# Moving the constants behind a weight tile, shortening the zero products, and eight more pairs by seven products in an fp32 hybrid block

## The chip, the cores and the metric

The kernel runs on one core of one Trainium2 chip. The metric is the device time of one execution in microseconds, the median over runs; lower is better. The core has a matrix engine (TensorE; PE in the profile, its weight loads PEld), a vector engine (VectorE, DVE), a scalar engine (ScalarE, ACT), GpSimd (POOL) and SyncE (SP), whose queue issues nearly all transfers from memory. Each engine works off its own instructions in a fixed order.

## The reference

One layer of a sequence model over 256 positions of width 2048, all in float32, cut to what matters:

```python
def rms_norm(x, w):
    y = x * rsqrt(mean(x * x, axis=-1, keepdims=True) + 1e-6)
    return y * w

def hybrid_token_mixer(n, w_in, ...):
    proj = n @ w_in            # 2048 x 8208: q, k, v, z, a, b of eight gated DeltaNet heads,
                               # q, f, i, g of eight HGRN2 heads
    y_a = gated_deltanet_group(...)   # short causal convolution, l2 norms, chunked delta rule, gated norm
    y_b = hgrn2_group(...)            # lower-bounded forget gate, chunkwise recurrence, gated norm
    return concatenate([y_a, y_b], axis=-1) @ w_out       # 2048 x 2048

def squared_relu_mlp(n, w1, w2):
    return square(relu(n @ w1)) @ w2                      # 2048 x 8192, 8192 x 2048

def reference(x, ...):
    h = x
    h = h + hybrid_token_mixer(rms_norm(h, norm_mix_w), ...)
    h = h + squared_relu_mlp(rms_norm(h, norm_ffn_w), w_ff1, w_ff2)
    return rms_norm(h, norm_final_w)
```

## The kernel before

**Products in three parts.** TensorE multiplies in a rounded float32 format (F32R). A float32 matrix is therefore split in two: `hi`, its rounded copy, made by a cast on ScalarE (L120), and `lo`, the remainder `w - hi`, made on VectorE (L121). A product is then three matmuls, hi x hi, lo x hi and hi x lo (L805, L806, L807). Every weight goes through `split` on its way from memory, so each weight tile of 128 x 2048 costs ScalarE two casts and VectorE two remainders of 128 x 1024.

**Start.** The parameters come by the queue of ScalarE, everything else by that of SP: `x` transposed in eight pieces (tile `big`) and the first two weight tiles in eight pieces, one after the other (L146, L147). While they travel, GpSimd sets 384 columns of `sums` to zero and TensorE multiplies zeros, eight products of 128 x 128 with 128 x 256 into the tile `warm` (L173 to L175). `to_T` (L167, L168) then makes `xT`, the hi and lo of `x` times the norm weight.

**Projections.** `project` makes two outputs of one head from two weight tiles, `kh` 0 and 1. The first call (`first`) uses the two tiles that are already on their way. The second call (`second`) loads its tile `kh` 0 in four pieces and then, before its tile `kh` 1, three constants: `cst`, which holds the identity and two columns (L297), `cst_a` with the ones, masks and selections (L298), and `wab`, the weights of the gates (L299). Weight tiles have three buffers (`wpool`). Between the second call's splits stand the squares of `x` (`squares`), and after them the row sums by a product with the ones (`row_scales`). `parameters` copies the ones into `ones_r` in F32R, and `gates` splits `wab` and multiplies it with `xT` (tile `pab`). Then the heads follow, projections of one head beside the mixing of the one before, up to about 490 us.

**MLP.** A step takes a pair of k-tiles: one weight tile of 128 x 2048, which is a 2 x 2 block of parts of 128 x 512, against a 2 x 2 block of activations of 128 x 128, for two halves of the positions and two of the columns. There are two kinds.

- A plain pair (`plain_quad`): eight products, 24 matmuls, added into four accumulators `E`. Its weights take two splits of 128 x 1024.
- A pair by sums (`sum_quad`): seven products of sums of the parts (a Strassen-Winograd scheme), 21 matmuls, added into three of the `E` and four further accumulators `M`. VectorE makes the sums of the weights in the tile `TT`, which has one buffer (L845, L848, L849), and there are three splits of 128 x 1024 and one of 128 x 512. After the last pair of this kind `joins` adds the `M` together into `C4` (L863 to L867).

The split weights of 128 x 1024 have five buffers in turn (`split_pair`: three of one pool, two of another). The accumulators are the eight banks of PSUM, four of `acc_a` and four of `acc_b`; a group has its `E` in the one and its `M` in the other, and the next group the other way round.

The first product has eight groups `ng` of 1024 columns, each with eight pairs `kp`, three of them by sums (`SUMS`, pairs 2, 4 and 6). Its activations are made once: `blocks(kp, ...)` transposes a pair's part of `h` and writes either the plain hi and lo (`a_plain`) or the seven sums' hi and lo (`a_sums`). At a group's end VectorE adds each `E` to its part of `C4` (L906) and ScalarE takes the Relu (L907). Four `turn`s, one per quarter, then transpose these results (L817) and square them into `g` (L819). They wait in the list `fills` and are put between the next group's products: `fill(2)` after pair 0, and two in the middle of pair 1. The transposes go to banks of the pool that held the group's `E`, which is the pool of the next group's `M`.

The second product has two halves `q` of 1024 columns, each with 32 pairs, six of them by sums (`SUMS2`, pairs 3, 7, 11, 15, 19 and 23). The splits of `g` are made pair by pair (`a2_plain`, `a2_sums`). After the last pair by sums come `joins` and four additions into `h` (`add_to_h`), in the second half also the weighting of half of the first rows of the output (`weighted`). The last two pairs of a half are held and worked off accumulator by accumulator (`finish`), and the final norm is made piece by piece behind them.

**What sets the order.** The program text gives the priority, and a scheduler with a cost model writes each engine's order from it ahead of the run: an instruction that is lower in the text goes ahead where the model has the engine idle. On the chip each engine keeps to that order.

Of the kernel before, what the change touches and what calls it, by code (L numbers as in the profile page):

```python
# [15 lines left out]
P = 128  # L16
T = 256
# [58 lines left out]
def hybrid_block(ctx: ExitStack, tc: tile.TileContext, x, xt, w_in, w_ab, params, w_out, w_ff1, w_ff2,  # L76
# [93 lines left out]


    warm = mx("warm")
    POOL.memset(sums[:, 0:P + T], 0.0)  # L173
    for _ in range(8):
        PE.matmul(warm[:, 0:T], lhsT=sums[:, 0:P], rhs=sums[:, P:P + T], start=True, stop=True)  # L175

    for k in range(KT):
        to_T(xT, k, x3[:, k, :], cols[:, k:k + 1])

    def squares(c, after):  # L180

        t = junk if c else sums
        DVE.tensor_copy(t[:, 0:1], after)
        ACT.activation(t, big[:, c * 1024:(c + 1) * 1024], AF.Square)
        if c:
            DVE.tensor_tensor(out=sums, in0=sums, in1=junk, op=ALU.add)

    def row_scales():

# [14 lines left out]
        ACT.activation(u, u, AF.Exp, scale=-1.0)  # L204
        ACT.activation(u, u, AF.Ln, bias=1.0)

    ones_r = cpool.tile([P, P], F32R, tag="ones_r", name="ones_r")

    def parameters():

        DVE.tensor_copy(ones_r, ones)
        l0, l1 = cols[:, 34:42], cols[:, 42:50]
        DVE.tensor_tensor(out=par[:, 2, :], in0=l0, in1=l1, op=ALU.max)
        DVE.tensor_tensor(out=par[:, 3, :], in0=l0, in1=par[:, 2, :], op=ALU.subtract)
        DVE.tensor_tensor(out=par[:, 4, :], in0=l1, in1=par[:, 2, :], op=ALU.subtract)
        ACT.activation(par[:, 3:5, :], par[:, 3:5, :], AF.Exp)
        DVE.tensor_tensor(out=par[:, 5, :], in0=par[:, 3, :], in1=par[:, 4, :], op=ALU.add)
        DVE.reciprocal(par[:, 5, :], par[:, 5, :])
        DVE.tensor_tensor(out=lb, in0=par[:, 3, :], in1=par[:, 5, :], op=ALU.mult)
        DVE.tensor_scalar(oml, lb, -1.0, 1.0, ALU.mult, ALU.add)  # L220
        DVE.tensor_scalar(gnw[:, 0:1], cols[:, 32:33], float(P) ** -0.5, None, ALU.mult)
        DVE.tensor_copy(gnw[:, 1:2], cols[:, 33:34])
# [61 lines left out]
    def project(base, hd, chunk, dsts):  # L284
        second = base == 0 and hd == 0 and chunk == 1
        accs = [acc_a() for _ in range(2)]
        for kh in range(2):
            first = base == 0 and hd == 0 and chunk == 0
            if first:
                w = w_first[kh]  # L290
            else:
                w = wtile()
                src = w_in[((base > 0) * NH + hd) * 4 + chunk * 2 + kh]
                if second and kh == 0:
                    for c in range(4):
                        SP.dma_start(w[:, c * 512:(c + 1) * 512], src[:, c * 512:(c + 1) * 512])
                    SP.dma_start(cst, consts[:, 0:NKEEP])  # L297
                    SP.dma_start(cst_a, consts[:, NKEEP:])  # L298
                    SP.dma_start(wab, w_ab)  # L299
                else:  # L300
                    SP.dma_start(w, src)
            for q in range(2):
                hi, lo = split(w[:, q * 1024:(q + 1) * 1024], 1024, pieces=2 if first or second and kh == 0 else 1)
                if second:
                    squares(2 * kh + q, lo[:, 0:1].bitcast(F32))
                hi = hi.rearrange("p (k g c) -> p k g c", k=4, g=2)
                lo = lo.rearrange("p (k g c) -> p k g c", k=4, g=2)
                for kk in range(4):
                    k = kh * 8 + q * 4 + kk
                    for g in range(2):  # L310
                        PE.matmul(accs[g], lhsT=hi[:, kk, g, :], rhs=xT[:, k, :], start=(k == 0), stop=False)  # L311
                        PE.matmul(accs[g][:, T:], lhsT=lo[:, kk, g, :], rhs=xT[:, k, 0:T],  # L312
                                  start=False, stop=(k == KT - 1))
# [394 lines left out]


    KP = KT // 2  # L710
    SUMS = (2, 4, 6)
    sets = bpool.tile([P, 8192], F32R, tag="xT", name="sets")
    sets2 = tp.tile([P, 2 * 1792], F32R, tag="s2", name="sets2")
    plain = [kp for kp in range(KP) if kp not in SUMS]

    def a_plain(kp):
        n = plain.index(kp)
        return sets[:, n * 1024:(n + 1) * 1024].rearrange("p (k s) -> p k s", k=2)

    def a_sums(kp):  # L720
        t, at = (sets, 6144) if kp == SUMS[0] else (sets2, (SUMS.index(kp) - 1) * 1792)
        return t[:, at:at + 1792].rearrange("p (s n t) -> p s n t", s=2, n=7)

    h = hpool.tile([P, 2 * D], F32, tag="h", name="h").rearrange("p (f c) -> p f c", f=2)
# [14 lines left out]
    def blocks(kp, acc):  # L739
# [7 lines left out]
        if kp in plain:  # L747
            for kk in range(2):
                to_T(a_plain(kp), kk, pt[:, kk * T:(kk + 1) * T], wc[kk])
            return  # L750

        X = op.tile([P, 8, P], F32, tag="X", name="X", bufs=2)
# [118 lines left out]
    for ng in range(NGR):  # L871
# [2 lines left out]
        bank_e, bank_m = (acc_a, acc_b) if ng % 2 == 0 else (acc_b, acc_a)  # L874
        E = [bank_e() for _ in range(4)]
        M = None
        for kp in range(KP):
            w = wtile()
            SP.dma_start(w, w_ff1[ng * KP + kp])
            if kp not in SUMS:  # L880
                st = a_plain(kp)
                plain_quad(E, lambda kk, hf: [st[:, kk, c + hf * P:c + hf * P + P] for c in (0, T)], plain_weights(w),
                           kp == 0, kp == KP - 1, 0 if kp == 0 else 2)
                if kp == 0:
                    fill(2)
                if ng == 0 and kp == 1:
                    for hf in range(2):
                        DVE.tensor_tensor(out=fs[:, 4 + hf:5 + hf], in0=fs[:, 2 * hf:2 * hf + 1],
# [9 lines left out]
            if M is None:  # L898
                M = [bank_m() for _ in range(4)]
            st = a_sums(kp)  # L900
            sum_quad(E, M, [(st[:, 0, n, :], st[:, 1, n, :]) for n in range(7)], w, kp == SUMS[0], kp == SUMS[-1])
            if kp == SUMS[-1]:
                C4 = joins(M)

        for at, p in ((0, E[0]), (2, E[1]), (1, E[2]), (3, E[3])):
# [45 lines left out]
            DVE.tensor_scalar(h[:, hf, a:b], o[hf][:, a:b], s, None, ALU.mult)  # L951
        (ACT if eng is ACT else SP).dma_start(out[0, hf * P:(hf + 1) * P, a:b], h[:, hf, a:b])

    SUMS2 = (3, 7, 11, 15, 19, 23)
    TAIL = 2
    KP2 = NF // 2

# [142 lines left out]
```

## Time and profile before

| | |
|---|---|
| median of 3 runs | 1238.5 us (1237.87 to 1238.79) |
| profiled execution | 1239.85 us |
| its span, first to last instruction | 1238.1 us |
| granted TensorE clock, mean | 0.993 |
| TensorE busy | 1219.7 us, 7076 matmuls |
| VectorE busy | 1022.4 us |
| ScalarE busy | 767.2 us |
| GpSimd busy | 135.3 us |
| moved by transfers | 233.46 MB, 189 GB/s on average |

Rows of the profile name an engine, a line of the kernel, an operation and its tiles, written `out<-in`. In a list by time the first number is the start in microseconds from the span's start, the second the duration; `x2` says that two were merged. In brackets stands how long the engine had been idle, and what ended that. A row of the stretches gives, after its length, the busy time and count of instructions of TensorE, its weight loads, VectorE, ScalarE and GpSimd, then the granted clock, the share of the transfer engines and their GB/s. In lists of groups the two numbers behind the bar are the time in which at least one of the group ran, in us, and the mean duration in ns. In lists of waits they are the total in us, how often, and the longest.

### The profile page before, as it was taken

To read this page: it belongs to the slowest core of one execution; us is meant where nothing else is said; L and a number is where in the kernel's file an instruction comes from. 1 tells how busy PE (TensorE), PEld (TensorE's weight loads), DVE (VectorE), ACT (ScalarE), POOL (GpSimd) and SP (SyncE) were. 2 spreads that over 40 slices of the span, in tenths; PEclk is the share of its full clock that TensorE was granted. 3 is DMA by queue.
4 is the path that set the end of the run, shared out by engine and by line. 5 is a ranking of instruction groups with operands and counts; after the bars stand their busy time and mean duration, and the time that the engine had idled before them with its cause. 6 is when DMAs were issued, how large, how long until landed. Compare 5 with 4: busy or idle time off the path is not lost.

```text
span 1238.1 us, 18475 instructions
## 1 busy us (share of the span) xinstructions
PE 1219.7 (99%) x7076; PEld 1023.5 (83%) x7076; DVE 1022.4 (83%) x1421; ACT 767.2 (62%) x1073; POOL 135.3 (11%) x185
## 2 busy tenths in 40 slices
PE   8999999998999999999999999999999999999997
PEld 7888888887888887888888888888888888888886
DVE  6789899888789996778898898889888786887874
ACT  6666767665667765565666566566566564656553
POOL 0142444262111111000000000000000000000000
PEclk9999999998999999999999999999999999999998
DMA  8455555544335445655555555565765555564651
GB/s 318 154 152 174 185 192 186 177 148 140 112 129 216 168 170 180 231 194 204 204 184 209 201 178 182 202 204 184 268 228 204 204 204 203 181 220 174 227 186 68
DMA packets 37144, 233.46 MB, mean 189 GB/s; under 512 B 4696, under 2 KB 5728, under 8 KB 10176
## 3 DMA queue, kind: packets, MB, share of 16 engines
q1 hardware_dynamic: 34848, 229.83, 52.8%
q0 software_dynamic: 1632, 1.72, 0.9%
q8 instruction: 55, 0.90, 0.3%
q10 hardware_dynamic: 576, 0.74, 0.2%
q14 instruction: 33, 0.27, 0.1%
HBM read 227.67 MB, written 4.60 MB: 188 GB/s over the span
## 4 chain that ended last, share of the span: by engine, by line
PE 89%; DVE 4%; DMA 2%; issue 2%; POOL 2%; ACT 1%; SPq 0%; POOLq 0%; ACTq 0%; DVEq 0%
PE acc L311 14%; PE acc L807 9%; PE acc L806 9%; PE acc L805 9%; PE accb L806 9%; PE accb L807 9%; PE accb L805 9%; PE acc L312 7%; PE accb L776 4%; PE acc L776 4%; DVE lo L121 1%; DMA w<-in_w_in_dram 1%; POOL X L458 1%; PE acc L817 1%; PE accb L817 1%
## 5 line engine op out<-in xcount | busy, mean ns | idle before, releaser
L121 DVE TENSOR_TENSOR lo<-w,hi 128x1024 fp32r<-128x1024 f32 (+1 forms) x422 | 492.3, 1174 | 129.9 <-ACT hi L120 121.3
L120 ACT CAST hi<-w 128x1024 fp32r<-128x1024 f32 (+1 forms) x422 | 420.3, 1001 | 262.8 <-PE acc L806 64.7
L311 PE MATMUL acc<-xT,hi 128*128 128x512 f32 x1024 | 359.9, 398 | 1.4 <-ACT hi L120 1.4
L312 PE MATMUL acc<-xT,lo 128*128 128x256 f32 x1024 | 280.8, 284 | 1.1 <-DVE lo L121 1.1
L311 PEld LDWEIGHTS acc<-xT,hi 128*128 128x128 f32 x1024 | 189.7, 189 | 40.5 <-ACT hi L120 1.7
L312 PEld LDWEIGHTS acc<-xT,lo 128*128 128x128 f32 x1024 | 193.4, 190 | 8.2 <-DVE lo L121 2.9
L121 DVE TENSOR_TENSOR lo<-TT,hi 128x1024 fp32r<-128x1024 f32 x72 | 87.3, 1223 | 28.0 <-ACT hi L120 25.0
L120 ACT CAST hi<-TT 128x1024 fp32r<-128x1024 f32 x72 | 75.0, 1052 | 42.5 <-PE acc L806 14.1
L806 PE MATMUL accb<-hi,sets 128*128 128x512 f32 x244 | 95.4, 391 | 0.0
L806 PE MATMUL acc<-hi,sets 128*128 128x512 f32 x244 | 95.3, 391 | 0.0
L805 PE MATMUL acc<-hi,sets 128*128 128x512 f32 x244 | 95.0, 391 | 0.0
L805 PE MATMUL accb<-hi,sets 128*128 128x512 f32 x244 | 94.7, 391 | 0.0
L807 PE MATMUL acc<-lo,sets 128*128 128x512 f32 x244 | 93.5, 391 | 0.0
L807 PE MATMUL accb<-lo,sets 128*128 128x512 f32 x244 | 93.5, 391 | 0.0
L806 PE MATMUL acc<-hi,gs 128*128 128x512 f32 (+1 forms) x216 | 83.3, 386 | 0.0
L805 PE MATMUL acc<-hi,gs 128*128 128x512 f32 (+1 forms) x216 | 83.0, 386 | 0.0
L943 POOL TENSOR_TENSOR fin<-fin,cst 128x1 f32<-128x1 f32 x2 | 1.1, 564 | 747.6 <-DVE fin L942 747.6
L807 PE MATMUL acc<-lo,gs 128*128 128x512 f32 (+1 forms) x216 | 81.9, 385 | 0.0
L806 PE MATMUL accb<-hi,gs 128*128 128x512 f32 x204 | 79.4, 389 | 0.0
L805 PE MATMUL accb<-hi,gs 128*128 128x512 f32 x204 | 78.7, 389 | 0.0
L807 PE MATMUL accb<-lo,gs 128*128 128x512 f32 x204 | 78.7, 389 | 0.0
L805 PEld LDWEIGHTS accb<-hi,sets 128*128 128x128 f32 x244 | 45.8, 188 | 9.4
(335 smaller groups left out, 1978.2 us busy)
## 6 DMA issues: line engine op xcount, KB each, us to landing
w<-in_w_ff_dram SPq DMA_DIRECT2D x128, 1024.0 KB, 4.9
w<-in_w_in_dram SPq DMA_DIRECT2D x61, 1024.0 KB, 4.9
w<-in_w_out_dram SPq DMA_DIRECT2D x16, 1024.0 KB, 4.9
w<-in_w_in_dram SPq DMA_DIRECT2D x12, 256.0 KB, 5.4
big<-in_xt_dram SPq DMA_DIRECT2D x8, 256.0 KB, 5.5
h<-in_x_dram SPq DMA_DIRECT2D x2, 1024.0 KB, 5.8
scr_h<-h SPq DMA_DIRECT2D x4, 512.0 KB, 5.8
tail<-scr_h SPq DMA_DIRECT2D x2, 1024.0 KB, 6.0
```

The source lines that it names most:

```text
L120: ACT.copy(hi, w)
L121: eng.tensor_tensor(out=lo, in0=w, in1=hi.bitcast(F32), op=ALU.subtract)
L311: PE.matmul(accs[g], lhsT=hi[:, kk, g, :], rhs=xT[:, k, :], start=(k == 0), stop=False)
L312: PE.matmul(accs[g][:, T:], lhsT=lo[:, kk, g, :], rhs=xT[:, k, 0:T], start=False, stop=(k == KT - 1))
L458: POOL.tensor_tensor(out=X[:, j + 1:, 0:ncol], in0=X[:, j + 1:, 0:ncol], in1=t3, op=ALU.subtract)
L776: PE.matmul(accs[2 * hf + c], lhsT=st, rhs=ww[:, c * 512:(c + 1) * 512], start=(k == 0 and a == 0 and ww is hi), stop=(k == 2 * NH - 1 and ...
L805: PE.matmul(dst, lhsT=ah, rhs=bh, start=start, stop=False)
L806: PE.matmul(dst, lhsT=al, rhs=bh, start=False, stop=False)
L807: PE.matmul(dst, lhsT=ah, rhs=bl, start=False, stop=stop)
L817: PE.transpose(pt[:, c * P:(c + 1) * P], src[:, c * P:(c + 1) * P], ident)
L943: POOL.tensor_tensor(out=r, in0=r, in1=C("nhalf"), op=ALU.pow)
```

## The change

Three edits stand together.

1. The three constants are issued on SP's queue behind the second call's tile `kh` 1 instead of before it. The copy of the ones into `ones_r` moves from `parameters` into `squares`, behind the last remainder of the second call; a copy of one column of that remainder holds it there.
2. The zero products at the start are eleven of 128 columns instead of eight of 256, and GpSimd clears 128 columns instead of 384.
3. More pairs are by sums. In the first product the odd groups have four, pairs 1, 2, 4 and 6; `blocks` makes both forms of pair 1's activations, and `sets2` holds three sets instead of two. In these groups all four `turn`s follow pair 0. In the second product each half has eight, pairs 3, 7, 10, 14, 17, 21, 24 and 28.

```diff
-    POOL.memset(sums[:, 0:P + T], 0.0)
-    for _ in range(8):
-        PE.matmul(warm[:, 0:T], lhsT=sums[:, 0:P], rhs=sums[:, P:P + T], start=True, stop=True)
+    POOL.memset(sums[:, 0:P], 0.0)
+    for _ in range(11):
+        PE.matmul(warm[:, 0:P], lhsT=sums[:, 0:P], rhs=sums[:, 0:P], start=True, stop=True)
...
     def squares(c, after):
...
             DVE.tensor_tensor(out=sums, in0=sums, in1=junk, op=ALU.add)
+        if c == 3:
+            DVE.tensor_copy(ones_r[:, 0:1], after)
+            DVE.tensor_copy(ones_r, ones)
...
     def parameters():
-        DVE.tensor_copy(ones_r, ones)
...
                 if second and kh == 0:
                     for c in range(4):
                         SP.dma_start(w[:, c * 512:(c + 1) * 512], src[:, c * 512:(c + 1) * 512])
+                else:
+                    SP.dma_start(w, src)
+                if second and kh == 1:
                     SP.dma_start(cst, consts[:, 0:NKEEP])
                     SP.dma_start(cst_a, consts[:, NKEEP:])
                     SP.dma_start(wab, w_ab)
-                else:
-                    SP.dma_start(w, src)
...
-    SUMS = (2, 4, 6)
+    SUMS = ((2, 4, 6), (1, 2, 4, 6))
+    WITH_SUMS = (2, 1, 4, 6)
     sets = bpool.tile([P, 8192], F32R, tag="xT", name="sets")
-    sets2 = tp.tile([P, 2 * 1792], F32R, tag="s2", name="sets2")
-    plain = [kp for kp in range(KP) if kp not in SUMS]
+    sets2 = tp.tile([P, 3 * 1792], F32R, tag="s2", name="sets2")
+    plain = [kp for kp in range(KP) if kp not in SUMS[0]]
...
     def a_sums(kp):
-        t, at = (sets, 6144) if kp == SUMS[0] else (sets2, (SUMS.index(kp) - 1) * 1792)
+        n = WITH_SUMS.index(kp)
+        t, at = (sets2, (n - 1) * 1792) if n else (sets, 6144)
...
         if kp in plain:
             for kk in range(2):
                 to_T(a_plain(kp), kk, pt[:, kk * T:(kk + 1) * T], wc[kk])
+        if kp not in WITH_SUMS:
             return
...
+        with_sums = SUMS[ng % 2]
         for kp in range(KP):
...
-            if kp not in SUMS:
+            if kp not in with_sums:
...
                 if kp == 0:
-                    fill(2)
+                    fill(4 if 1 in with_sums else 2)
...
-            sum_quad(E, M, [...], w, kp == SUMS[0], kp == SUMS[-1])
-            if kp == SUMS[-1]:
+            sum_quad(E, M, [...], w, kp == with_sums[0],
+                     kp == with_sums[-1])
+            if kp == with_sums[-1]:
                 C4 = joins(M)
...
-    SUMS2 = (3, 7, 11, 15, 19, 23)
+    SUMS2 = (3, 7, 10, 14, 17, 21, 24, 28)
```

More of the change, by code (lines that the diff above doesn't have):

```diff
@@ L172, in hybrid_block @@
     warm = mx("warm")
-    POOL.memset(sums[:, 0:P + T], 0.0)
-    for _ in range(8):
-        PE.matmul(warm[:, 0:T], lhsT=sums[:, 0:P], rhs=sums[:, P:P + T], start=True, stop=True)
+    POOL.memset(sums[:, 0:P], 0.0)
+    for _ in range(11):
+        PE.matmul(warm[:, 0:P], lhsT=sums[:, 0:P], rhs=sums[:, 0:P], start=True, stop=True)
     for k in range(KT):
         to_T(xT, k, x3[:, k, :], cols[:, k:k + 1])
+    ones_r = cpool.tile([P, P], F32R, tag="ones_r", name="ones_r")
     def squares(c, after):
@@ L205, in sigmoid_parts @@
         ACT.activation(u, u, AF.Ln, bias=1.0)
-    ones_r = cpool.tile([P, P], F32R, tag="ones_r", name="ones_r")
     def parameters():
-        DVE.tensor_copy(ones_r, ones)
         l0, l1 = cols[:, 34:42], cols[:, 42:50]
@@ L900, in hybrid_block @@
             st = a_sums(kp)
-            sum_quad(E, M, [(st[:, 0, n, :], st[:, 1, n, :]) for n in range(7)], w, kp == SUMS[0], kp == SUMS[-1])
-            if kp == SUMS[-1]:
+            sum_quad(E, M, [(st[:, 0, n, :], st[:, 1, n, :]) for n in range(7)], w, kp == with_sums[0],
+                     kp == with_sums[-1])
+            if kp == with_sums[-1]:
                 C4 = joins(M)
```

## The prediction

> **What bounds the kernel now.** I read the page first (engines, then the chain that ended last), then busy time by stretch, then the waits of each engine, then the two places that the edit touches in order of time.
>
> ```profile
> span 1238.1 us, 18475 instructions
> PE 1219.7 (99%) x7076; PEld 1023.5 (83%) x7076; DVE 1022.4 (83%) x1421; ACT 767.2 (62%) x1073; POOL 135.3 (11%) x185
> ...
> PE 89%; DVE 4%; DMA 2%; issue 2%; POOL 2%; ACT 1%; SPq 0%; POOLq 0%; ACTq 0%; DVEq 0%
> ...
> core 0: us, PE busy (x) PEld busy (x) DVE busy (x) ACT busy (x) POOL busy (x), PEclk, DMA share, GB/s
> ...
> 20.00:25.00 5.00, 4.40 (x26) 3.59 (x24) 2.11 (x4) 1.96 (x5) 0.00 (x0) 1.00 1.02 413
> ...
> 492.00:551.00 59.00, 58.25 (x273) 48.56 (x274) 41.77 (x58) 33.51 (x46) 0.00 (x0) 1.00 0.66 231
> ...
> 594.60:638.00 43.40, 43.40 (x202) 36.00 (x201) 36.96 (x40) 26.28 (x31) 0.00 (x0) 1.00 0.55 194
> ...
> 911.00:1065.00 154.00, 154.00 (x681) 127.52 (x680) 122.05 (x155) 89.02 (x113) 0.00 (x0) 1.00 0.55 193
> ...
> DVE lo L121 <- ACT hi L120: 95.4, 103, 1.7
> ```
>
> The chain is TensorE for 89% of the span. A stretch as long as one group of the first MLP product (43.4 us) and the first half of the second (154 us) have TensorE busy all through, so in the MLP a removed matmul is removed time, as long as VectorE keeps up: it is busy 37.0 of 43.4 us. The last row is the VectorE waits between 551 and 1222 us: 95.4 us behind ScalarE's casts. Those waits cost nothing today.
>
> **The products by sums.** A plain pair is 8 products of 3 matmuls (24), a pair by sums 7 (21). Four groups (1, 3, 5, 7) turn one more pair, each half of the second product turns two more: 4 + 4 = 8 pairs, 24 matmuls fewer. Their pace:
>
> ```profile
> 685.04 0.39 PE L805 MATMUL acc<-hi,sets 128*128 128x512 f32 x1
> ...
> 689.80 0.39 PE L805 MATMUL accb<-hi,sets 128*128 128x512 f32 x1
> ```
>
> These are the first and last of 22 matmuls in a row: 4.76 us over 21 steps, 0.2267 us each (the 0.39 us durations overlap). 24 x 0.2267 = **5.4 us less** on TensorE.
>
> What it adds on VectorE, from the rows by form:
>
> ```profile
> L121 DVE TENSOR_TENSOR lo<-w,hi 128x1024 fp32r<-128x1024 f32 x374 | 460.3, 1237 | 128.5 <-ACT hi L120 120.6 <-PE poh L669 1.4 <-PE accb L817 0.7
> ...
> L121 DVE TENSOR_TENSOR lo<-TT,hi 128x1024 fp32r<-128x1024 f32 x72 | 87.3, 1223 | 28.0 <-ACT hi L120 25.0 <-PE accb L745 1.3
> ...
> L845 DVE TENSOR_TENSOR TT<-w 128x1024 f32<-128x1024 f32 x36 | 44.0, 1221 | 5.5 <-DMA w<-in_w_ff_dram 5.1
> ...
> L121 DVE TENSOR_TENSOR lo<-w,hi 128x512 fp32r<-128x512 f32 x48 | 32.6, 683 | 1.4 <-PE accb L807 0.7 <-ACT hi L120 0.7
> ...
> L848 DVE TENSOR_TENSOR TT<-w,TT 128x512 f32<-128x512 f32 x36 | 24.7, 686 | 0.5
> ```
>
> Busy over count: a plain pair is two 1024-wide remainders, 2 x 1.23 = 2.46 us. A pair by sums is one of them, two of TT (2 x 1.21), the wide difference 1.22, two narrow ones (2 x 0.69) and a 512-wide remainder 0.68: 6.93 us. So 4.5 us more per turned pair. A group with four such pairs has 37.0 + 4.5 = 41.5 us of VectorE against 43.4 - 3 x 0.2267 = 42.7 us of TensorE: 1.2 us to spare, where there were 6.4. In a half of the second product two pairs add 9.0 us and the sums of their activations; even at 18 us in all it would be 140 of 154 - 1.4 = 152.6 us, which hides. ScalarE has room in both (26.3 of 43.4, 89 of 154).
>
> So the first product's odd groups are the doubtful place, at their beginning, because now the second pair is by sums too, and the third after it. What is late there is the end of the group before:
>
> ```profile
> 709.10 0.58 ACT L863 COPY C<-acc 128x512 f32<-128x512 f32 x1
> ...
> 717.75 1.88 DVE L906 TENSOR_TENSOR C<-accb,C 128x512 f32<-128x512 f32 x3
> ...
> 718.47 1.83 ACT L907 ACTIVATE C<-C 128x512 f32<-128x512 f32 x3 [2.37 <-DVE C L906]
> ...
> 594.64 0.87 PE acc L817 x8
> ```
>
> The sixth pair's copy at 709.10 follows its last matmul, so the plain pair 7 (24 x 0.2267 = 5.4 us) ends near 714.5 and the next group's pair 0 near 719.9. The four results' last additions on VectorE run until 719.6, over 5 us behind TensorE, since weight work stands between them in its order; the Relus end at 720.3. Today only two turns follow pair 0, the other two come in the middle of pair 1. With the change all four follow pair 0 (16 transposes, 1.74 us by the row of eight): the fourth needs its Relu by about 719.9 + 1.3 = 721.2, which leaves 0.9 us. After that the four banks of turns become M of pair 1, 1.4 us into it at the earliest. One remainder (1.2 us) more ahead of the additions makes TensorE wait 0.3 us, two make it wait 1.5. The shared TT tile adds a like risk: pair 2's difference has to wait until pair 1's are split. Bounds per odd group: 0, and all the ScalarE waits that a group has now, 95.4 / 671 x 43.4 = 6.2 us, less 1.2 to spare = 5.0. I take 0.5 us, near the low end, since those waits today are mostly VectorE that has caught up with its buffers: 4 x 0.5 = **2.0 us given back**.
>
> At nothing I put: pair 1's own sums (four small additions and one remainder under 1024 wide, before the MLP, where VectorE is busy 41.8 of 59 us); the longer SUMS2 list's joins, now at pair 28 of 32. They take about 6.7 us of VectorE (four joins at 0.68 us, four additions to h as wide, in the second half a weighting as wide as a remainder) and stand ahead of pairs 30 and 31, needed within 6.8 us. Before, at pair 23, they were spread out among the remainders:
>
> ```profile
> 1188.85 0.68 DVE L865 TENSOR_TENSOR C<-acc,C 128x512 f32<-128x512 f32 x1
> 1189.84 1.23 DVE L121 TENSOR_TENSOR lo<-w,hi 128x1024 fp32r<-128x1024 f32 x1 [0.32 <-ACT hi L120]
> ```
>
> If that order holds it hides; if the joins go first, each half loses up to 2 us (one activation remainder 0.7 and one of weights 1.2 come after 6.8). I take 0 and keep 4 us for the range.
>
> **Later constants.** In order of time, SP's issues, then TensorE:
>
> ```profile
> 13.76 0.33 SPq L297 DMA_DIRECT2D cst<-in_consts_dram  x1
> ...
> 15.11 0.33 SPq L299 DMA_DIRECT2D wab<-in_w_ab_dram  x1
> ...
> 15.85 8.73 DMA w<-in_w_in_dram
> 24.66 1.05 ACT hi L120
> 25.74 1.24 DVE lo L121
> 27.02 0.80 PE acc L312 x2
> ...
> 24.12 0.28 PE L312 MATMUL acc<-xT,lo 128*128 128x256 f32 x1
> ...
> 30.60 0.39 PE L311 MATMUL acc<-xT,hi 128*128 128x512 f32 x1
> ...
> 27.00:30.00 3.00, 2.98 (x10) 2.60 (x11) 1.82 (x4) 1.06 (x1) 0.00 (x0) 0.50 0.43 87
> ...
> cst_a<-in_consts_dram SPq DMA_DIRECT2D x1, 619.5 KB, 5.8
> ...
> wab<-in_w_ab_dram SPq DMA_DIRECT2D x1, 128.0 KB, 5.5
> ...
> cst<-in_consts_dram SPq DMA_DIRECT2D x1, 65.0 KB, 4.9
> ...
> 26.56 0.40 ACT L120 CAST ab<-wab 128x256 fp32r<-128x256 f32 x1
> ...
> 42.74 3.69 PE pab L233 x16
> ```
>
> This weight tile (second chunk, second half) is on the chain from its issue to 27.02. TensorE has run out at 24.35 and, when the tile is there, runs at half clock from 27 to 30 us. By 30.60 seven pairs of matmuls (one of 512, one of 256 columns) are done; at full pace, 1.5 x 0.2267 = 0.34 us a pair, they would end 2.4 us after 24.35, at 26.8: 3.8 us lost. Now the tile is issued at 13.76, in the place of the first constant. The constants are 65 + 620 + 128 = 813 KB; at 413 GB/s they took 2.0 us of full queues (the earlier issue is 2.1 us too). So the tile lands at 24.58 - 2.0 = 22.5, its cast ends at 23.6, its remainder at 24.9; TensorE waits 0.5 us instead, which I take as too short to lose the clock, since it took a gap of 1.4 us and a second wait before, and is through seven pairs at 24.9 + 2.1 = 27.0, not 30.6: **3.6 us less**. Bounds: 0, if the transfers share the queues so that it lands no earlier; 3.8. I take the high end, since wab, the last that was issued before the tile, also landed well before it (15.11 + 5.5 = 20.6). The tile moves past three issues on SP's queue; the constants move back by one issue (0.7 us) each and by the tile's transfer, and land by about 24.6, as the same bytes lie ahead. Their first use is wab's cast, at 26.6 before; the ones' first use, the row sums, stands just ahead of the gates' matmuls at 42.7, and their cast, now behind the fourth square on VectorE, is 128 columns wide: nothing.
>
> **Short zero products.**
>
> ```profile
> 1.26 6.27 PE L175 MATMUL warm<-sums 128*128 128x256 f32 x16 [1.26 <-POOL pre L346]
> ...
> 7.18 0.81 PE L311 MATMUL acc<-xT,hi 128*128 128x512 f32 x2
> ...
> 5.80 0.69 DVE L121 TENSOR_TENSOR lo<-w,hi 128x512 fp32r<-128x512 f32 x1
> ...
> 8.34 0.69 DVE L121 TENSOR_TENSOR lo<-w,hi 128x512 fp32r<-128x512 f32 x1 [0.67 <-ACT hi L120]
> ```
>
> Each of 8 products is two records, 16 in 6.27 us. 11 of half the width: 6.27 x 11 / 16 = 4.3 us. The first real matmul then comes when its remainder is there, at 6.5 and not 7.2, but the second piece's remainder ends at 9.03 as before, held up by its weights, and by then TensorE has caught up in both cases: **0**, between a gain of 0.7 and the loss of rival A.
>
> **Sum.** -5.4 + 2.0 - 3.6 = -7.0 us. The profiled execution took 1239.85 us (span 1238.1, 1.75 around it), 0.1% above the median of 1238.5; I take the difference off the median: **1231.5 us**.
>
> **Rivals.** A: the clock. The row of 27 to 30 us shows what a gap does here: half clock for 3 us. A shorter start that leaves TensorE idle before 9 us could bring the same there. The Trainium skill ("TensorE: Matmul & The Clock Gate", "The HAM clock gate") says that full clock is granted after one busy free-running window of about 3.4 us; by that rule 4.3 us of zero products need not fill a whole window, which 6.3 us nearly always do; the trace agrees on the length of the slow stretch, and no run here shows the shorter start. Priced by rows: 3 us at half pace lose 1.5 us, of which 0.5 is covered by the tile's wait: 1.0 us worse, 1232.5. Chance 8%.
>
> B: the tile lands no earlier: 1231.5 + 3.6 = 1235.1. For it: several transfers are in flight at once; against it: landings in order. 10%.
>
> C: VectorE eats the MLP gain, at the odd groups or at pairs 28 to 31: 2 to 5 us more than I took, 1233.5 to 1237. 16%.
>
> D, the other side: VectorE becomes the bound of the odd groups. Its waits stay as they are, on top of more work: 41.5 + 6.2 = 47.7 against 43.4 now, +4.3 x 4 = 17 us; less the second product's 2.7 and 3.6 at the start: 1249. It ends slower than before from the point where more than 1.2 + (5.4 + 3.6) / 4 = 3.5 us of the 6.2 remain in each odd group. For it: one TT tile, a strict order. Against: TensorE never waited with three such pairs. 8%.
>
> **Chances.** My forecast (1229.3 to 1233.5) 56%, A 8, B 10, C 16, D 8, 2 for what I don't see. 0.2% is 2.5 us, about what can be told from no change here: faster below 1236.0, slower above 1241.0. Faster: 56 + 8 + 9 + 10 = 83%; same 9%; slower 8%. The low end is all gains and nothing given back, 1238.5 - 9.2 = 1229.3, with a little; the high end takes in B and C: 1229.0 to 1237.0.
>
> **What would show it.** The tile landing near 22.5, no half clock at 27 to 30 us and the gates' matmuls (at 42.7 before) near 39.1: step right. An odd group of 42.7 us and TensorE without a wait: nothing given back; a wait of the transposes on C or of remainders on ScalarE near pairs 0 to 2: the 2.0. TensorE waits after pair 28: C. VectorE over 42 us busy in 43: D. The forecast is wrong if the order on VectorE changes so that additions stand far behind weight work.

## The result, and the profile after

The changed kernel takes 1230.38 us (median of 6 runs, 1229.82 to 1231.41) against 1238.64 us before (6 runs, 1237.83 to 1239.94): ratio 0.9933, 95% interval 0.992 to 0.9946, so 6.7 to 9.9 us faster. The prediction was 1231.5. The profiled execution of the changed kernel took 1230.59 us.

The page of the changed kernel: span, busy time of the engines, the chain by engine.

```profile
span 1228.9 us, 18515 instructions
PE 1211.9 (99%) x7058; PEld 1018.8 (83%) x7058; DVE 1054.7 (86%) x1487; ACT 777.1 (63%) x1096; POOL 136.2 (11%) x185
...
PE 93%; POOL 2%; DVE 2%; DMA 1%; issue 1%; ACT 0%; POOLq 0%; SPq 0%; DVEq 0%
```

TensorE holds 93% of the chain instead of 89. VectorE is 32.3 us busier and TensorE still does not wait for it: the list of TensorE's waits is empty for the MLP, as it was before.

**The start.** The landing of the second call's tile `kh` 1, issue to landing, in the changed kernel and then in the kernel before:

```profile
L300 SPq DMA_DIRECT2D w<-in_w_in_dram x1: 328/328/328, 13.8 to 13.8; - x1
...
DMA to landing us min/median/max: 7.2/7.2/7.2
```

```profile
L301 SPq DMA_DIRECT2D w<-in_w_in_dram x1: 328/328/328, 15.8 to 15.8; - x1
...
  ACT hi L120: 3.0, 1
...
DMA to landing us min/median/max: 8.7/8.7/8.7
```

Issued 2.0 us earlier and 1.5 us shorter on its way, the tile lands at 21.05 us instead of 24.58; ScalarE, which waited 3.0 us for it, no longer does. The stretches of the changed kernel (busy time and count of TensorE, its weight loads, VectorE, ScalarE, GpSimd, then the granted clock):

```profile
20.00:25.00 5.00, 5.00 (x31) 4.37 (x30) 3.85 (x5) 4.33 (x6) 0.00 (x0) 1.00 1.04 407
...
27.00:30.00 3.00, 3.00 (x19) 2.65 (x18) 2.88 (x4) 2.14 (x3) 0.00 (x0) 1.00 0.84 344
```

TensorE is busy all through and at full clock, where the kernel before had 10 matmuls at a clock of 0.50 from 27 to 30 us. The gates' matmuls (`pab`) begin at 35.7 us, where the prediction looked for 39.1:

```profile
L235 PE MATMUL pab<-xT,ab x16: 387/394/585, 35.7 to 39.4; 128*32 128x512 f32 x16
```

That is not all time gained. In TensorE's order they now stand behind 80 matmuls of the projections with `hi` instead of 88, so they were moved forward as well.

**The MLP.** An even and an odd group (2 and 3) of the changed kernel, the second with four pairs by sums:

```profile
623.30:666.60 43.30, 43.30 (x200) 35.98 (x199) 38.54 (x44) 25.68 (x32) 0.00 (x0) 1.00 0.57 206
666.60:709.26 42.66, 42.66 (x198) 35.41 (x196) 36.79 (x41) 27.52 (x34) 0.00 (x0) 1.00 0.54 200
```

The odd group takes 42.66 us, what its matmuls alone need (the prediction's 42.7), and VectorE is busy for 36.8 us of it and 38.5 of the even one beside it. The MLP from its first to its last product is 688.68 us before and 683.05 after.

### The profile page after: what moved, and what is told of

Read it like the earlier page. It is cut to its first block, busy times and chain, and to the rows that moved or that the text cites. A ratio compares the mean times of both kernels' runs of the same rounds, so it can differ in the third digit from the quotient of the medians.

```text
span 1228.9 us, 18515 instructions
## 1 busy us (share of the span) xinstructions
PE 1211.9 (99%) x7058; PEld 1018.8 (83%) x7058; DVE 1054.7 (86%) x1487; ACT 777.1 (63%) x1096; POOL 136.2 (11%) x185
## 4 chain that ended last, share of the span: by engine, by line
PE 93%; POOL 2%; DVE 2%; DMA 1%; issue 1%; ACT 0%; POOLq 0%; SPq 0%; DVEq 0%
PE acc L314 17%; PE acc L812 9%; PE acc L811 9%; PE acc L813 9%; PE acc L315 9%; PE accb L811 9%; PE accb L812 9%; PE accb L813 9%; PE accb L782 4%; PE acc L782 4%; POOL X L461 1%; PE acc L823 1%; PE accb L823 1%; PE pk L402 1%; DMA X<-scr_a 1%
## 5 line engine op out<-in xcount | busy, mean ns | idle before, releaser
L120 ACT CAST hi<-w 128x1024 fp32r<-128x1024 f32 (+1 forms) x422 | 413.2, 993 | 210.1 <-PE acc L812 55.6
L120 ACT CAST hi<-TT 128x1024 fp32r<-128x1024 f32 x88 | 92.0, 1052 | 77.5 <-issue 21.7
L121 DVE TENSOR_TENSOR lo<-TT,hi 128x1024 fp32r<-128x1024 f32 x88 | 106.9, 1222 | 30.3 <-ACT hi L120 27.4
L811 PE MATMUL acc<-hi,sets 128*128 128x512 f32 x260 | 101.5, 392 | 0.0
L812 PE MATMUL acc<-hi,sets 128*128 128x512 f32 x260 | 101.3, 390 | 0.0
L811 PE MATMUL accb<-hi,sets 128*128 128x512 f32 x224 | 88.1, 393 | 0.0
L812 PE MATMUL accb<-hi,sets 128*128 128x512 f32 x224 | 87.4, 390 | 0.0
L813 PE MATMUL accb<-lo,sets 128*128 128x512 f32 x224 | 78.8, 392 | 0.0
L812 PE MATMUL acc<-hi,gs 128*128 128x512 f32 (+1 forms) x200 | 77.1, 385 | 0.0
L811 PE MATMUL acc<-hi,gs 128*128 128x512 f32 (+1 forms) x200 | 76.8, 386 | 0.0
L813 PE MATMUL acc<-lo,gs 128*128 128x512 f32 (+1 forms) x200 | 75.7, 386 | 0.0
L812 PE MATMUL accb<-hi,gs 128*128 128x512 f32 x188 | 73.2, 390 | 0.0
L811 PE MATMUL accb<-hi,gs 128*128 128x512 f32 x188 | 72.8, 390 | 0.0
L851 DVE TENSOR_TENSOR TT<-w 128x1024 f32<-128x1024 f32 x44 | 53.7, 1220 | 5.9 <-DMA w<-in_w_ff_dram 5.9
```

The lines of the kernel that those rows point to most:

```text
L120: ACT.copy(hi, w)
L121: eng.tensor_tensor(out=lo, in0=w, in1=hi.bitcast(F32), op=ALU.subtract)
L811: PE.matmul(dst, lhsT=ah, rhs=bh, start=start, stop=False)
L812: PE.matmul(dst, lhsT=al, rhs=bh, start=False, stop=False)
L813: PE.matmul(dst, lhsT=ah, rhs=bl, start=False, stop=stop)
L851: DVE.tensor_tensor(out=TT[:, 0:1024].rearrange("p (a c) -> p a c", a=2), in0=view(w, 0, [[1536, 2], [1, 512]]), in1=view(w, 512, [[-512, ...
```

## The experiments

All are compared by five landmarks in their traces, starts of TensorE's instructions. "Start" is from the 45th to the 65th matmul `acc<-xT,hi` of the projections, around the late tile; "heads" from the 65th to the 329th; "solve" from the 713th to the 761st, around the solve of the DeltaNet blocks at 285 to 300 us; "out" from the first product of the output projection to the first of the MLP; "MLP" from its first to its last product. In us, one profiled execution each:

| kernel | start | heads | solve | out | MLP |
|---|---|---|---|---|---|
| before | 10.90 | 107.41 | 36.91 | 97.36 | 688.68 |
| changed | 7.00 | 106.31 | 36.65 | 98.92 | 683.05 |
| b_const | 7.00 | 106.31 | 42.98 | 97.40 | 688.68 |
| b_zero | 9.56 | 107.15 | 42.33 | 97.39 | 688.68 |
| b_start | 7.00 | 106.67 | 36.86 | 98.94 | 688.68 |
| b_sums1 | 7.88 | 106.76 | 36.30 | 99.00 | 685.77 |
| b_sums2 | 9.77 | 106.86 | 37.06 | 99.00 | 685.96 |
| b_const_pin | 7.00 | 106.60 | 41.27 | 97.88 | 700.75 |
| a_all4 | 7.00 | 106.31 | 36.59 | 97.36 | 683.69 |
| a_45 | 7.00 | 106.31 | 36.58 | 99.00 | 705.96 |
| a_load2 | 7.00 | 108.10 | 37.09 | 97.37 | 683.72 |
| a_nozero | 7.00 | 106.31 | 37.91 | 98.99 | 684.11 |
| a_nine | 7.00 | 107.01 | 37.36 | 97.30 | 683.82 |
| a_nine_fill | 7.00 | 108.69 | 35.72 | 99.42 | 694.18 |

In "out", 98.9 to 99.0 instead of 97.4 is a half clock of 3.41 us at about 490 us, which six of these executions have. It is not tied to a kernel: the mean clocks of the changed kernel's six runs go from 0.993 (the profiled one) to 0.996, so most of them lost less of it.

### Each part alone

**b_const**, the constants behind the tile, with the copy of the ones that belongs to it, nothing else:

```diff
...
+                else:
+                    SP.dma_start(w, src)
+                if second and kh == 1:
                     SP.dma_start(cst, consts[:, 0:NKEEP])
                     SP.dma_start(cst_a, consts[:, NKEEP:])
                     SP.dma_start(wab, w_ab)
...
```

> The kernel before with the later constants alone. Theory: the weight tile lands at about 21.05 us instead of 24.58, TensorE's start-up loses 3.85 us of waiting and half clock, as in the changed kernel; if the 1.1 us that the changed kernel gains between 75 and 140 us hangs on the same edit, 4.95 us in all: 1238.6 - 3.9 to - 5.0 = 1233.7 to 1234.8. Rival (tile lands no earlier in itself, the gain needs the short zero products too): 0 to -1 us, 1237.6 to 1238.6. Rival on the head stage (the 1.1 us come from the short zero products or from chance in the order): -3.85 us and the chain at 98 to 138 us still on VectorE and ScalarE.

Measured: 1239.13 us (11 runs) against 1238.43; ratio 1.0004, 0.9996 to 1.0013, no change that can be told. In the trace the start gains its 3.9 us and the solve loses 6.1. That execution took 1241.54 us, the longest of the eleven (from 1237.79), with a mean clock of 0.991; one other has 0.991 (1241.2 us), and the nine with 0.993 or 0.994 took 1237.8 to 1239.6. So the loss is not as large in all of them.

**b_zero**, the short zero products alone:

```diff
-    for _ in range(8):
-        PE.matmul(warm[:, 0:T], lhsT=sums[:, 0:P], rhs=sums[:, P:P + T], ...)
+    for _ in range(11):
+        PE.matmul(warm[:, 0:P], lhsT=sums[:, 0:P], rhs=sums[:, 0:P], ...)
```

> The kernel before with the short zero products alone. Theory: 0 us (within 0.4), 1238.6: the first real matmul comes 1.4 us earlier (5.75 for 7.18 us) but the third piece's at 10.18 us as before, and the wait and half clock at 24 to 30 us stay. Rival A (the clock after a shorter start): +1.0 us or more, with a half clock ahead of 10 us. Second rival: the 11 products move the end of the full-clock stretch, so that the half clock of 27 to 30 us goes or moves: -1 to -2 us.

Measured: 1241.17 us (11 runs), ratio 1.0022, 1.0011 to 1.0034: slower, but by the solve (+5.4 us in the trace, an execution of 1244.53 us), not by a clock lost ahead of 10 us: the clock's records have full clock from 5.32 us.

**b_sums1**, four pairs by sums in the odd groups alone (`SUMS = ((2, 4, 6), (1, 2, 4, 6))` and what belongs to it):

> The kernel before with four of eight pairs by seven products in the odd groups of the first MLP product, and nothing else. Theory (nothing given back): 4 groups x 3 x 0.2267 = -2.72 us, 1235.9, odd groups 42.65 us without a wait of TensorE. Prediction's own step (0.5 us given back in each): -0.7 us, 1237.9. Rival D (VectorE the bound): slower, above 1241.

Measured: 1235.39 us (7 runs), ratio 0.9976, 0.9965 to 0.9986, so 1.7 to 4.3 us faster; the MLP 2.91 us shorter. An odd group of it:

```profile
582.76:625.38 42.62, 42.62 (x197) 35.44 (x196) 37.21 (x42) 26.75 (x34) 0.00 (x0) 1.00 0.51 184
```

Nothing is given back.

**b_sums2**, the longer list `SUMS2` alone:

> The kernel before with eight pairs by seven products in each half of the second MLP product, and nothing else. Theory (joins at pair 28 hide): 2 halves x 2 x 3 x 0.2267 = -2.72 us, 1235.9. Rival C (joins ahead of pairs 30 and 31 make TensorE wait): up to 2 us lost in each half, so -2.7 to +1.3 us.

Measured: 1237.46 us (11 runs), ratio 0.9989, 0.998 to 0.9998. The MLP is 2.72 us shorter, exactly the matmuls, so the joins at pair 28 cost nothing. The median moved by 1.0 us only; the interval reaches to 2.5, and the profiled execution had a half clock at 493 us that the one of before has not.

The four parts alone add up to +0.7 + 2.7 - 3.0 - 1.0 = -0.6 us, the change is -8.3. So the parts are not independent, and the table says where: "solve".

### What happens at the solve

What TensorE waits for from 284 to 302 us (total, times, longest), first in the changed kernel, then in b_const:

```profile
PE pd L638 <- issue: 1.9, 1, 1.9
PE pP L513 <- DVE Xn L492: 0.9, 1, 0.9
```

```profile
PE pP L513 <- DVE Xn L492: 5.5, 1, 5.5
```

The wait is for one addition of the solve on VectorE. VectorE in order of time, first the changed kernel, then b_const:

```profile
294.54 1.22 DVE L121 TENSOR_TENSOR lo<-w,hi 128x1024 fp32r<-128x1024 f32 x1
295.67 0.41 DVE L492 TENSOR_TENSOR Xn<-pQ,Xn 128x256 f32<-128x256 f32 x1
```

```profile
295.36 1.23 DVE L121 TENSOR_TENSOR lo<-w,hi 128x1024 fp32r<-128x1024 f32 x1 [0.37 <-ACT hi L120]
296.98 0.42 DVE L582 SCALAR_TENSOR_TENSOR u<-R,u 128x256 f32<-128x256 f32 x1 [0.39 <-ACT u L210]
297.44 0.96 DVE L583 SCALAR_TENSOR_TENSOR u<-R,u 128x768 f32<-128x768 f32 x1
298.32 0.42 DVE L492 TENSOR_TENSOR Xn<-pQ,Xn 128x256 f32<-128x256 f32 x1
```

And ScalarE, again the changed kernel first:

```profile
290.26 1.04 ACT L120 CAST hi<-w 128x1024 fp32r<-128x1024 f32 x1
293.18 0.84 ACT L208 ACTIVATE u<-R 128x768 f32<-128x768 f32 x1 [1.89 <-DVE R L328]
```

```profile
293.55 0.84 ACT L208 ACTIVATE u<-R 128x768 f32<-128x768 f32 x1 [2.82 <-DVE R L328]
294.30 1.03 ACT L120 CAST hi<-w 128x1024 fp32r<-128x1024 f32 x1
```

Two things stand in another order, written ahead of the run by the scheduler's model: ScalarE's second cast of a weight tile behind a gate's activation instead of ahead of it, and two of the gate's operations on VectorE ahead of the solve's addition. The addition is 2.65 us later (2.4, counted from the 713th product of the projections), and TensorE idles. In this execution what follows costs more than that again. The stretch from 296 to 313 us in the changed kernel and in b_const:

```profile
296.00:313.00 17.00, 16.79 (x267) 14.95 (x268) 15.80 (x35) 11.13 (x23) 4.01 (x5) 0.84 0.34 119
```

```profile
296.00:313.00 17.00, 14.21 (x214) 12.51 (x215) 13.90 (x31) 9.12 (x19) 2.95 (x5) 0.51 0.14 56
```

The half clock lasts 17.07 us by the clock's records, not 6.83. b_zero has the same order and the same 17.07 us. The order is part of the kernel; how long the clock is lost need not be the same in every execution. A third kernel with this order, a_nozero (below), shows the two apart. It has the wait, and its stretch from 296 to 313 us has a clock of 0.80:

```profile
PE pP L513 <- DVE Xn L492: 5.3, 1, 5.3
```

```profile
296.00:313.00 17.00, 15.31 (x249) 13.41 (x250) 14.30 (x32) 9.51 (x20) 4.28 (x5) 0.80 0.29 105
```

Its half clock lasts 6.83 us, and its solve takes 37.91 us, 1.3 more than the changed kernel's, with the addition 1.0 us later counted from the 713th product. So in that execution the order alone cost about what the addition was late, and the rest of b_const's and b_zero's loss goes with the longer half clock. Two more kernels were to test the order.

**b_start**, the two edits of the start together (both diffs above); in its order the addition stands ahead of the gate's operations:

> The kernel before with the later constants and the short zero products together, no change in the MLP. Each of them alone brought 0 and +2.7 us, since in both VectorE's addition of the solve (Xn<-pQ,Xn) had slid behind two gate operations (u<-R,u) that wait for ScalarE, TensorE waited 5.5 us and ran at half clock for 17 us behind it. In this kernel the addition stands ahead of the gate operations again, as in the kernel before and the changed one. Theory (order at the solve decides): the start's gain of 3.9 to 4.9 us comes whole, 1233.5 to 1234.6, and the step from the projection's matmul 712 to 760 takes about 36.9 us, not 42 to 43. Rival (the two edits' own costs add up): 0.7 + 2.7 = +3.4 us, 1241.9.

Measured: 1236.47 us (11 runs) against 1238.12; ratio 0.9983, 0.9974 to 0.9992. The solve takes 36.86 us, as the theory had it, and the two edits together are faster where each alone is not. The gain is smaller than expected, 1.0 to 3.2 us instead of 3.9 to 4.9; a reason is below, in the start's own step. Between b_start (-1.65 us) and b_const (+0.7) lie 2.4 us, between b_start's zero products (0 in the start) and b_zero 2.7: in medians too the order costs about what the addition is late. That is 5.1 of the 7.7 us that the parts' sum is short of the change. The other 2.6 stay open: b_sums2's median gained 1.7 us less than its MLP, and b_start's 1.0 less than the change gained outside the MLP.

**b_const_pin**, b_const with the addition held ahead of the gate's operations:

```diff
         DVE.tensor_tensor(out=Xn[:, :, 0:HB], in0=pq[1], in1=Xn[:, :, 0:HB], op=ALU.add)
+        DVE.tensor_copy(solved, Xn[:, 0, 0:1])
...
         sigmoid_parts(u[:, 0:3, :], R[:, 0:3, :], 3 * T)
+        if hd == SOLVE_AT - NH + 1:
+            DVE.tensor_copy(u[:, 3, 0:1], solved)
```

> The kernel before with the later constants alone, and the solve's addition held ahead of the next head's gate operations on VectorE by two copies of one column (one out of the sum, one into the tile that the gate operation then overwrites). Theory (order at the solve): the gain of the start shows, 1233.5 to 1234.9, TensorE's wait for the addition falls from 5.5 us to about 1. Rival (what the later constants cost lies elsewhere, in the constants' late landing or in the clock): as without the copies, 1238.5 to 1239.5.

Measured: 1251.26 us (4 runs), ratio 1.0104, 1.009 to 1.0119: much slower. The solve itself went from 42.98 to 41.27 us and the wait for the addition from 5.5 to 3.7: the two gate operations were part of it. The cast on ScalarE, which the copies don't move, still stands behind the gate's activation and may be the rest; the half clock is again 17.07 us. The slowdown is elsewhere, in the MLP, 700.75 us instead of 688.68 with the same matmuls and no wait of TensorE. The first and the last of 19 matmuls in a row there:

```profile
699.75 0.39 PE L813 MATMUL acc<-hi,sets 128*128 128x512 f32 x1
...
703.92 0.40 PE L813 MATMUL accb<-hi,sets 128*128 128x512 f32 x1
```

4.17 us over 18 steps, 0.2317 us each, where the prediction's row of before had 0.2267, at full clock in both. `solved` is a tile of 4 bytes in each partition, in the pool that the program opens first. The other kernel with it, a_nine_fill, has the slow pace too, the twelve others have 0.2267. That the tile shifts the weights' addresses, and that this is the cause, is inferred; no run without the shift was made. So this kernel does not decide the question as a whole. b_start speaks for the order: with the addition in its old place the loss is gone, as it is in every trace with that order. But no kernel changes the order and nothing else, so its price in medians is inferred.

### How much VectorE can still take

**a_all4**, four pairs by sums in groups 1 to 7, `with_sums = SUMS[min(ng, 1)]`:

> The changed kernel with four pairs by seven products (1, 2, 4, 6) in groups 1 to 7 of the first MLP product, not in the odd ones alone; group 0 keeps three. Theory (VectorE keeps up by itself in every group, 41.5 of 42.7 us): 3 more groups x 3 x 0.2267 = -2.04 us, 1228.3. Rival (VectorE lives on the lighter groups between, and its remaining waits on ScalarE, 66.1 us of 678, 4.2 us a group, do not go): 3 us per group short from the second heavy group on, 1230.4 - 2 + 6 x 3 = 1246.

Measured: 1231.41 us (5 runs) against 1238.55; ratio 0.9942, 0.9929 to 0.9954, no better than the changed kernel. Two groups of it:

```profile
665.50:708.60 43.10, 43.02 (x198) 35.35 (x197) 39.72 (x45) 26.73 (x33) 0.00 (x0) 1.00 0.55 195
708.60:751.70 43.10, 43.02 (x198) 35.34 (x197) 39.72 (x45) 26.73 (x33) 0.00 (x0) 1.00 0.55 195
```

Neither theory: heavy groups (those with four pairs by sums) one after the other take 43.10 us each, 0.43 more than their matmuls, so three groups win 0.24 and three lose 0.43. The 0.4 us lies at the last turn: the weight load of its transposes (L823) waits 0.5 us for the last Relu (ACT, L915). A fourth heavy pair has VectorE busy for 39.7 us, not for the 41.5 that I had worked out.

**a_45**, four pairs by sums in the even groups and five in the odd, `SUMS = ((2, 4, 5, 6), (1, 2, 4, 5, 6))`:

> The changed kernel with one more pair by seven products in every group of the first MLP product: pairs 2, 4, 5, 6 in the even groups and 1, 2, 4, 5, 6 in the odd ones. TensorE: 8 x 3 x 0.2267 = 5.4 us less, groups of 42.67 and 42.0 us. VectorE by the prediction's prices: 41.5 and 46.0 us, mean 43.75. Theory (VectorE's busy time is the bound from here, its waits on ScalarE go to near nothing): groups of 43.75 us on the mean, against 43.0 now, 8 x 0.75 = +6 us, less some of it for the last group's slack: 1234 to 1237. Rival D's price (the remaining waits of 4.2 us a group stay on top): 48 us a group, +40 us, 1270. Rival (VectorE's order lets it carry over more than it seems): -5.4 us, 1225.

Measured: 1254.48 us (4 runs), ratio 1.0127, 1.0114 to 1.0141. An odd group and what TensorE waits for in the MLP:

```profile
581.66:628.95 47.29, 43.94 (x194) 34.31 (x193) 45.78 (x52) 29.28 (x36) 0.00 (x0) 1.00 0.50 170
```

```profile
PE acc L811 <- ACT hi L120: 7.4, 7, 1.9
PE accb L811 <- ACT hi L120: 1.9, 6, 0.5
```

Here VectorE is the bound, busy for 45.8 of 47.3 us. TensorE's longest waits are put down to ScalarE's casts; that these in turn wait for buffers that VectorE frees late is my reading and was not tested. The MLP is 22.9 us longer: between the two prices expected.

**a_load2**, the wide difference of the weights made twice in pairs 2 and 4 of the odd groups:

```diff
+        for _ in range(times):
             DVE.tensor_tensor(out=TT[:, 0:1024].rearrange("p (a c) -> p a c", a=2), in0=..., in1=..., op=ALU.subtract)
```

> The changed kernel, with the wide difference of the weights (VectorE, 128x1024, 1.22 us) made twice in pairs 2 and 4 of the odd groups; the second writes the same values. VectorE has 2.44 us more, 43.95 us in odd groups of 42.67. Theory (the even groups, 37.0 of 43.35 us, take over what is late, through the five weight buffers): within 1 us of the changed kernel, 1230.4 to 1231.4. Rival (each group has to carry itself): 1.3 us x 4 = +5 us, 1235.6. Rival D's reading (the remaining waits of 4.2 us stay): VectorE at 41.5 + 4.2 = 45.7 would already have shown a wait, so that all of 2.44 x 4 = 9.8 us appears: 1240.

Measured: 1232.09 us (5 runs), ratio 0.9946, 0.9934 to 0.9958. The MLP is 0.67 us longer for 8 x 1.22 = 9.8 us more work. An odd group of it:

```profile
581.62:624.25 42.63, 42.63 (x198) 35.42 (x196) 39.76 (x44) 26.95 (x34) 0.00 (x0) 1.00 0.52 182
```

The even groups carry nearly all of it, as the theory said: here VectorE's waits were spare time as long as a lighter group stood between. The 0.67 us lie in one odd group (43.35 us, from 753.55).

### The clock

**a_nozero**, one zero product instead of eleven:

> The changed kernel with one zero product of 128 columns instead of eleven. Theory from rival A's rule: without the zero products TensorE is too little busy ahead of 6 us, full clock comes a window of about 3.4 us later (at 7.8 us or later instead of 4.4), and the first pieces' matmuls run at half pace: 0 to 1.7 us lost, as far as the pieces' own waits up to 10.2 us do not hide it: 1230.4 to 1232.1. Rival (the clock does not hang on them): 0.

Measured: 1232.57 us (5 runs), ratio 0.9949, 0.9936 to 0.9963, some 2 us slower than the changed kernel, though the intervals overlap. The clock did come later: the records have full clock from 9.59 us, where the changed kernel has it from 4.38, and until then the same matmul takes 0.63 us instead of 0.40:

```profile
7.46 0.63 PE L314 MATMUL acc<-xT,hi 128*128 128x512 f32 x1
...
9.94 0.40 PE L314 MATMUL acc<-xT,hi 128*128 128x512 f32 x1
```

So the zero products do bring the full clock forward. But its loss is covered by the waits for the first pieces: the 45th product begins at 23.28 us (22.89 in the changed kernel, 23.31 in a_all4, which has all eleven) and the next 20 take 7.00 us. The loss is in the solve (37.91 for 36.65, the order of b_const again) and in the MLP (684.11 for 683.05, group 7). Rival A's mechanism shows here, its price of 1.0 us does not.

**a_nine**, `SUMS2 = (3, 6, 9, 12, 15, 18, 21, 24, 27)`:

> The changed kernel with nine pairs by seven products in each half of the second MLP product, 3, 6, 9 and so on to 27. Theory (VectorE hides: 14.9 us for three pairs against 15.65 of TensorE): 2 x 3 x 0.2267 = -1.36 us, MLP 681.7 us long instead of 683.05, 1229.0. Rival (VectorE is the bound in each three pairs): 9 x 2 x 0.5 to 1 us lost, slower than the changed kernel by 5 us and more.

Measured: 1230.78 us (5 runs), ratio 0.9939, 0.9926 to 0.9953, not to be told from the changed kernel. The first half of the second product is the 0.68 us shorter that its three matmuls make (169.81 for 170.49); the second half keeps 0.9 us of waiting and group 7 is 1.2 us longer. TensorE's waits in the MLP:

```profile
PE accb L813 <- DVE lo L121: 0.8, 2, 0.6
PE acc L823 <- ACT C L915: 0.4, 1, 0.4
```

**a_nine_fill**, a_nine with TensorE kept busy in two gaps (results not used), and the two copies of b_const_pin:

```diff
+        for _ in range(20):
+            PE.matmul(pQ[:, 0:T], lhsT=ones_r, rhs=xT[:, 0, 0:T], start=True, stop=True)
...
         PE.matmul(pm, lhsT=ones_r, rhs=slo, start=False, stop=True)
+        if h0 == 2 * NH - 1:
+            for _ in range(18):
+                PE.matmul(pmb[:, T:2 * T], lhsT=ones_r, rhs=shi, start=True, stop=True)
```

> The kernel with nine pairs in each half, and TensorE kept busy in its two gaps of the head stage: 20 products of 128x128 with 128x256 behind the solve's second set of small products (into columns that nobody reads any more), with the solve's addition held in place as above, and 18 behind the last head's mean (into free columns of its bank). Their results are not used. Theory (half clock follows a window of about 3.4 us in which TensorE is busy for under some 0.55): no half clock at 295 and at 489 us, 2 to 3 us less from the first and 0 to 1.6 from the second, 1225 to 1227.5. Rival (half clock there hangs on something else, or the gaps are covered anyway): 1229, as without them. Second rival (the products stand in the way of the solve): slower than 1229.

Measured: 1243.27 us (5 runs), ratio 1.0042, 1.003 to 1.0055: slower, by the MLP's slow pace that came with the 4-byte tile (694.18 us). With the gaps filled no half clock comes in the head stage. From 296 to 313 us, a_nine and then a_nine_fill:

```profile
296.00:313.00 17.00, 15.56 (x247) 13.52 (x247) 15.64 (x33) 11.11 (x22) 4.17 (x6) 0.80 0.37 126
```

```profile
296.00:313.00 17.00, 15.38 (x329) 13.41 (x329) 16.15 (x32) 10.09 (x20) 2.86 (x4) 1.00 0.36 126
```

The solve takes 35.72 us for 37.36, a gain of 1.6. At 487 us the products stood in the way, the second rival:

```profile
487.24 2.27 PE L437 MATMUL pm<-shi,ones_r 128*128 128x256 f32 x18
...
490.98 1.20 PE L793 MATMUL accb<-hi,yTa 128*128 128x512 f32 x4 [1.47 <-DVE fsq L440]
```

```profile
489.55 0.47 ACT L438 ACTIVATE fsq<-pm,cst 128x256 f32<-128x256 f32 x1 [1.75 <-PE pm L437]
```

ScalarE reads columns 0 to 255 of the bank and waited for products into columns 256 to 511. The Trainium skill ("PSUM — Partial Sum Buffer", "PSUM bank collisions raise a hardware error") says that engines are to be ordered by bank and not by address; these rows agree.

## Why the prediction was right, and where it was not

The sum came out 1.1 us from the median because two of its terms were off in opposite directions; that it came so close is in part luck.

- **The MLP, -5.4 us:** right. The trace has -5.63, and the two halves alone -2.91 and -2.72.
- **Given back, 2.0 us:** wrong, it is 0. The step that failed is VectorE's budget, "37.0 + 4.5 = 41.5 us". The 37.0 was busy time, in which instructions that overlap count once; the 4.5 was in effect a sum of durations. VectorE's instructions start some 0.1 us before the one ahead ends when they do not wait (294.54 + 1.22 = 295.76 above, the next starts at 295.67). In durations a group went from 38.5 us before to 42.96 in a_all4, the 4.5 worked out; in busy time it went from 36.8 to 39.7. So 3 us were to spare, not 1.2, and a_load2 shows that a lighter group beside it gives more. The transposes' wait for the last Relu, for which I put the 0.5 us, came only where every group is heavy (0.43 us each in a_all4).
- **Joins at pair 28, 0:** right (b_sums2). No wait of TensorE stands in either half.
- **Later constants, -3.6 us:** the mechanism was right, the size was that of one execution. The tile lands at 21.05 us, even earlier than the 22.5 worked out; the predicted wait of 0.5 us does not come (TensorE ran out at 24.40 by the row of before, not at 24.35, which changes nothing), and the start takes 7.00 us in all ten kernels that have the edit. But without it the start takes 10.90, 9.56, 7.88 and 9.77 us: the old place let the tile's transfer take 7.2 us (b_sums1) to 9.1 (b_sums2), and only the profiled execution of before lost its clock as well. So the edit is worth 0.9 to 3.9 us by these executions. In medians it is the 1.7 us of b_start (1.0 to 3.2), or 8.3 less the MLP's 5.6, 2.6.
- **Short zero products, 0:** right for the start, and incomplete. Neither they nor the constants act only where they stand: each re-lays the written order of the head stage, and alone each seems to cost some 2.5 us at the solve (by medians; 5 to 6 in the profiled executions). That the changed kernel kept the good order there was not foreseen; the prediction had no term for it, so here it had luck.
- **Rivals.** A's loss did not come in b_zero, nor in a_nozero, where the full clock was 5 us late. B fell by the landing. C is 0 in the changed kernel. D did not come: VectorE's waits on ScalarE shrank from 95.4 to 65.8 us (551 to 1222 us) when there was more to do, as spare time does. TensorE waits for long only one pair by sums further, in a_45.

```profile
DVE lo L121 <- ACT hi L120: 65.8, 64, 2.4
```

None of the kernels beat the changed one beyond its interval. What the filling in the solve's gap would bring without the tile of 4 bytes, 1.6 us by the table, was not tried.

## What to carry to other kernels

Where a scheduler writes the order, a small edit can move a distant stage: compare the order and the landmarks of stages that the edit does not touch before a part is given credit or blame. Price an engine's budget in one currency, busy time with busy time, and read its waits as spare time until they reach the bounding engine. A start seen in one execution is one sample: here the same transfer, moved ahead, was worth 0.9 to 3.9 us.

## What the runs showed of the hardware

- **Half clock came after windows that were only in part idle.** The clock's records change in multiples of 3.41 us, at a phase that differs between executions. In the head stage TensorE was busy for 0 to 62% of the window of 3.41 us before each drop, while seven windows with 43 to 55% were not followed by one, so this share alone does not decide. The Trainium skill ("TensorE: Matmul & The Clock Gate", "The HAM clock gate") has the drop after an idle window; here a gap of some 2 us within it could be enough, and with 20 products in the gap none came (a_nine_fill, clock 1.00).
- **How long the half clock lasted did not go by the wait.** After waits of about the same length it lasted 17.07 us in b_const (5.5 us) and 6.83 in a_nozero (5.3). It lasted 17.07 us in the three executions in which TensorE was busy for 9 to 29% of the first 3.41 us at half clock (b_const, b_zero, b_const_pin), and 3.41 or 6.83 where it was busy for 54 to 100% of them. Why is not shown.
- **The pace of the same matmul.** 128x128 with 128x512 took 0.2267 us in twelve kernels and 0.2317 in the two that had a tile of 4 bytes ahead of the others, 10 to 12 us over the MLP. The cause is not shown.
